# Layer-norm statistics at the ends of sub-layers on ScalarE and GpSimd, and all weight splits on VectorE

## Chip, cores and metric
The kernel runs on one core of a Trainium2 chip. The metric is device microseconds of one execution, a median over several runs. A core has TensorE (PE, matrix products), VectorE (DVE), ScalarE (ACT) and GpSimd (POOL), each with its own instruction stream that runs in order, and SyncE (SP), which here starts the DMA transfers. An instruction waits on semaphores that the other engines raise.

## What is computed
An encoder of four layers over 512 tokens of width 1024, in float32. Each layer is a token mixer (multi-head latent attention MLA, retention, gated linear attention GLA, MLA again) and a SwiGLU FFN, and each of these eight sub-layers ends in a layer norm:

```python
def layer_norm(x, g, b):
    mu = jnp.mean(x, axis=-1, keepdims=True)
    var = jnp.mean(jnp.square(x - mu), axis=-1, keepdims=True)
    return (x - mu) * lax.rsqrt(var + LN_EPS) * g + b

for i in range(DEPTH):
    y = mixer[i % 3](x, ...)
    x = layer_norm(DEEPNORM_ALPHA * x + y, ln_g[i, 0], ln_b[i, 0])
    x = layer_norm(DEEPNORM_ALPHA * x + swiglu_ffn(x, ...), ln_g[i, 1], ln_b[i, 1])
```

## The kernel before
**Products.** A float32 product is made of three faster ones: each operand is split into a high half (rounded, a copy on ScalarE, L102) and a low half (the difference, a subtraction, L103), and `mm3` (L127 to L130) multiplies high by high, high by low and low by high. Weights stream from HBM in pieces of 128x1024 elements (`wraw`), which `wsplit` splits into `whi` and `wlo`. The activations `x` lie as four token tiles `xt0` to `xt3` of 128x1024, and transposed as `xh` and `xl`.

**End of a sub-layer.** `out_proj` makes the last projection tile by tile: for each token tile two halves of 512 columns, each summed in PSUM and added into `xt` by `acc` (L182 or L184). In the last pass `acc` also takes the statistics of the half (`bn_stats`, L186). When both halves are there, `ln_finish` aggregates them (L191), takes the reciprocal root of the variance in eight steps on 128x1 operands (`rsqrt`, L141 to L149; it can be given an engine, and GpSimd already runs it for the RMS norms), and normalises with two operations per half (L205, L206). In the tail (last layer) the second half of tiles 0 to 2 goes through ScalarE (L200) and GpSimd (L201, L202) and then out.

A finished tile is put on a list. `flush` takes it off later, in the middle of the products of a following tile: eight transposes on TensorE (L158), then `xh` on ScalarE and `xl` on VectorE. The next sub-layer begins with projections of these.

**Where weights are split.** After each end, `self.relieve = 6` makes the next six weight pieces have their low half computed by GpSimd; inside GLA there are three more times two. All others are on VectorE.

**Order.** The instructions of each engine are laid in an order by a scheduler when the program is built; the program's own order is only its input. So what stands in front of what is read from the built program. Buffers come from pools (`b=10` is the number of general 128x512 buffers in the FFN's phase).

Of the kernel before, what the change touches and what calls it, by code (L numbers as in the profile page):

```python
# [9 lines left out]
F32 = mybir.dt.float32  # L10
F32R = mybir.dt.float32r
I32 = mybir.dt.int32
AF = mybir.ActivationFunctionType
ALU = mybir.AluOpType
AX = mybir.AxisListType

P = 128
D = 1024
S = 512
NT = S // P  # L20
# [3 lines left out]
LN_EPS = 1e-5  # L24
# [26 lines left out]
class Trunk:  # L51
    def __init__(self, tc, ctx, ins, nb=47, nraw=3, nhl=6):
        self.tc, self.nc, self.ins = tc, tc.nc, ins
        nc = tc.nc
        ctx.enter_context(nc.allow_non_contiguous_dma(reason="rows of weights and broadcasts"))
        pool = lambda name, bufs, **k: ctx.enter_context(tc.tile_pool(name=name, bufs=bufs, **k))
        self.cp = pool("cp", 1)
        self.wp = pool("wp", 1)
        self.nb = nb
        self.sp = pool("sp", 8)  # L60
        self.lnp = pool("lnp", 2)

        xp = pool("xp", 1)
        self.xh = xp.tile([P, KT, S], F32R, name="xh")
        self.xl = xp.tile([P, KT, S], F32R, name="xl")
        self.ps_pool = pool("psum", 6, space=bass.MemoryType.PSUM)
        self.nraw, self.nhl = nraw, nhl
        self.relieve = 0
        self.pending = []
        self.waiting = []  # L70

        self.ident = self.cp.tile([P, P], F32, name="ident")
        make_identity(nc, self.ident)
        self.xt = [self.cp.tile([P, D], F32, name=f"xt{t}") for t in range(NT)]
# [23 lines left out]
        return self.b(shape, F32R, "bh", tag), self.b(shape, F32R, "bl", tag)  # L98


    def split(self, hi, lo, src, eng=None):
        a = self.nc.scalar.copy(hi, src)  # L102
        b = (eng or self.nc.vector).tensor_tensor(lo, src, hi.bitcast(F32), op=ALU.subtract)  # L103
        return a.ins, b.ins

    def wload(self, srcs, a, n):
# [9 lines left out]
    def wsplit(self, raw, a, n):  # L116
        hi = self.wp.tile([P, a, n], F32R, tag="whi", name="whi", bufs=self.nhl)
        lo = self.wp.tile([P, a, n], F32R, tag="wlo", name="wlo", bufs=self.nhl)
        self.split(hi, lo, raw, self.nc.gpsimd if self.relieve > 0 else None)
        self.relieve -= 1  # L120
        return hi, lo

    def wcols(self, w, r0, kt, c0, n):
# [46 lines left out]
    def ln_begin(self, i, k):  # L170
        nc = self.nc
        self.g = self.lnp.tile([P, D], F32, tag="ln", name="ln_g")
        self.bb = self.lnp.tile([P, D], F32, tag="ln", name="ln_b")
        nc.sync.dma_start(self.g, self.ins["ln_g"][i, k].partition_broadcast(P))
        nc.sync.dma_start(self.bb, self.ins["ln_b"][i, k].partition_broadcast(P))
        self.stats = [self.small(12, "lnst") for _ in range(NT)]

    def acc(self, t, half, ps, coef, last):
        nc = self.nc
        x = self.xt[t][:, half * 512 : half * 512 + 512]  # L180
        if coef is None:
            nc.vector.tensor_tensor(x, ps, x, op=ALU.add)  # L182
        else:
            nc.vector.scalar_tensor_tensor(x, x, coef, ps, op0=ALU.mult, op1=ALU.add)  # L184
        if last:
            nc.vector.bn_stats(self.stats[t][:, half * 6 : half * 6 + 6], x)  # L186

    def ln_finish(self, t, out=None):
        nc = self.nc
        mv = self.small(2, "lnmv")  # L190
        nc.vector.bn_aggr(mv, self.stats[t].rearrange("p (a b) -> p a b", b=6))  # L191
        r = self.rsqrt(mv[:, 1:2], 1.0, LN_EPS, "ln")
        x = self.xt[t]
        for hf in range(2):
            sl = slice(hf * 512, hf * 512 + 512)
            if out is not None and t < NT - 1 and hf == 1:

                nb = self.small(1, "lnnb")
                nc.vector.scalar_tensor_tensor(nb, mv[:, 0:1], -1.0, r, op0=ALU.mult, op1=ALU.mult)
                nc.scalar.activation(x[:, sl], x[:, sl], AF.Identity, bias=nb, scale=r)  # L200
                nc.gpsimd.tensor_tensor(x[:, sl], x[:, sl], self.g[:, sl], op=ALU.mult)  # L201
                nc.gpsimd.tensor_tensor(x[:, sl], x[:, sl], self.bb[:, sl], op=ALU.add)  # L202
                nc.sync.dma_start(out[t * P : (t + 1) * P, sl], x[:, sl])
                continue
            nc.vector.scalar_tensor_tensor(x[:, sl], x[:, sl], mv[:, 0:1], self.g[:, sl], op0=ALU.subtract, op1=ALU.mult)  # L205
            nc.vector.scalar_tensor_tensor(x[:, sl], x[:, sl], r, self.bb[:, sl], op0=ALU.mult, op1=ALU.add)  # L206
            if out is not None:
                nc.sync.dma_start(out[t * P : (t + 1) * P, sl], x[:, sl])
        if out is None:
            self.pending.append(t)  # L210


    def out_proj(self, st, w, nf, coef, last, out=None, halves=(0, 1)):
        wf = lambda f0, half: self.wcols(w, f0 * P, 2, half * 512, 512)
        if nf <= 6:
            ch = {(c, hf): wf(2 * c, hf) for hf in halves for c in range(nf // 2)}
            for t in range(NT):
                for hf in halves:
                    ps = self.ps()
                    for f in range(nf):  # L220
                        if last and hf == 0 and f == 3:
                            self.flush(t - 2)
                        w2 = ch[f // 2, hf]
                        self.mm3(ps, st(f, t), (w2[0][:, f % 2, :], w2[1][:, f % 2, :]), f == 0, f == nf - 1)
                    self.acc(t, hf, ps, coef, last)
                if last:
                    self.ln_finish(t, out)
            self.relieve = 6 if last else 0
            return
        pss = [self.ps() for _ in range(NT)]  # L230
        for f in range(nf):
            if f % 2 == 0:
                w2 = wf(f, 0)
            for t in range(NT):
                self.mm3(pss[t], st(f, t), (w2[0][:, f % 2, :], w2[1][:, f % 2, :]), f == 0, f == nf - 1)
        for t in range(NT):
            self.acc(t, 0, pss[t], coef, last)
        self.out_tail(st, lambda f0: wf(f0, 1), nf, coef, last, out)

    def out_tail(self, st, wf, nf, coef, last, out=None):  # L240

        pss = [self.ps() for _ in range(NT)]
        nl = 8
        for f in range(nf - nl):
            if f % 2 == 0:
                w2 = wf(f)
            for t in range(NT):
                self.mm3(pss[t], st(f, t), (w2[0][:, f % 2, :], w2[1][:, f % 2, :]), f == 0, False)
        ch = [wf(nf - nl + 2 * c) for c in range(nl // 2)]
        for t in range(NT):  # L250
            for c in range(nl):
                if last and c == 3:
                    self.flush(t - 2)
                f = nf - nl + c
                w2 = ch[c // 2]
                self.mm3(pss[t], st(f, t), (w2[0][:, c % 2, :], w2[1][:, c % 2, :]), f == 0, f == nf - 1)
            self.acc(t, 1, pss[t], coef, last)
            if last:
                self.ln_finish(t, out)
        self.relieve = 6  # L260


    def proj_f(self, w2, ps, kt, m, c=slice(None), mid=None):
# [674 lines left out]
    def gla(self, l, j):  # L938
        nc = self.nc
# [77 lines left out]
        def silu(r):  # L1017
            for x in r:
                self.silu = self.tc.keep_in_program_order(nc.scalar.activation(x, x, AF.Silu))
# [3 lines left out]
        v, r, hs = first()  # L1023
# [13 lines left out]
        for h in range(GLA_H):  # L1037
            at, states = self._gla_scores(c, keys, v, fwd, crs)
            if h < 2:
                if h:  # L1040
                    qk["q", h + 2] = q(h + 2)
                qk["k", h + 2] = k(h + 2)
            else:
                out(0, yT[:4], False, (h - 2,))
            self._gla_mix(at, states, c[2:], v, r, ng)
            r0 = r
            if h + 1 < GLA_H:
                cs = gates(h + 1)
                c = self._gla_chain(cs, qk["q", h + 1], qk["k", h + 1])
                (v,) = project(values(h + 1))  # L1050
            yT += self._gla_turn(r0)
            if h + 1 < GLA_H:
                (r,) = project(gate(h + 1))
                self.relieve = 2
                keys = self._gla_keys(c)
                silu(r)
        out(1, yT[4:], True)
# [192 lines left out]
    def run(self, out):  # L1250
        self.load_x(self.ins["x"][0])
        for i in range(DEPTH):
            self.mixer(i)
            with self.phase(fh=8, ft=1, t=3, u=1, b=10):
                self.ffn(i, out[0] if i == DEPTH - 1 else None)


# [38 lines left out]
```

## Time and profile before

| what | value |
|---|---|
| median of 3 runs | 2599.5 us (2598.32 to 2600.16) |
| the profiled execution | 2595.45 us |
| its span in the profile | 2593.7 us |
| mean granted TensorE clock | 0.994 |
| busy: PE, DVE, ACT, POOL | 2536.9, 1792.7, 974.6, 335.7 us |
| chain that ended last | PE 85%, DVE 9%, ACT 2%, POOL 2%, issue 2%, DMA 1% |

The span is from the first to the last instruction of the profiled execution. Busy shares are means over stages with different limits, so one reads next which instructions TensorE waited before, and then the timeline of the engine that it waited for. A row of a timeline gives the start, the duration, the engine and line, output and inputs, and in brackets the idle time ahead of it with what ended it.

### The profile page before, as it was taken

The page shows a single profiled execution, that of the slowest core. Times are in us where ns is not written, and L with a number is a line of the kernel's source. Part 1 is how long each engine was busy: PE and PEld are TensorE (multiplying, and loading weights), DVE is VectorE, ACT ScalarE, POOL GpSimd, SP SyncE. Part 2 cuts the span into 40 slices and gives each one's busy share as a digit, 9 for nine tenths or more (in the row PEclk, how much of TensorE's full clock was granted, in tenths as well). Part 3 has the DMA queues.
Part 4 walks back from the last instruction along what each step waited for, and adds up shares of the span by engine and source line. Part 5 has one row for each costly group of instructions (what it writes and reads, how often), then busy time and mean ns, then how long its engine had stood idle before and what let it go on. Part 6 is the DMA issues. An engine that isn't in the chain of part 4 may idle for free.

```text
span 2593.7 us, 32609 instructions
## 1 busy us (share of the span) xinstructions
PE 2536.9 (98%) x12804; PEld 2156.5 (83%) x12804; DVE 1792.7 (69%) x2900; ACT 974.6 (38%) x1405; POOL 335.7 (13%) x359
## 2 busy tenths in 40 slices
PE   8999999999999999999999999999999999999998
PEld 6888888887888887988888998888888788888887
DVE  6877666668755648566657878866657586666656
ACT  4652333323333332333323665233332464233331
POOL 3002111002100103111102001211102200211101
PEclk9999999999999999999999999999999999999999
DMA  4213333323222323333333222333333221333331
GB/s 147 74 42 94 106 98 98 106 74 103 76 81 82 98 80 88 108 93 107 110 95 88 76 66 74 110 98 98 98 90 86 61 77 44 120 98 98 98 90 57
DMA packets 294714, 232.36 MB, mean 90 GB/s; under 512 B 21120, under 2 KB 244480, under 8 KB 294560
## 3 DMA queue, kind: packets, MB, share of 16 engines
q1 hardware_dynamic: 294560, 230.28, 29.4%
q8 instruction: 100, 1.64, 0.3%
q14 instruction: 54, 0.44, 0.1%
HBM read 228.15 MB, written 2.10 MB: 89 GB/s over the span
## 4 chain that ended last, share of the span: by engine, by line
PE 85%; DVE 9%; ACT 2%; POOL 2%; issue 2%; DMA 1%; DVEq 0%; SPq 0%; ACTq 0%; POOLq 0%
PE ps L128 27%; PE ps L130 27%; PE ps L129 27%; DVE xt L205 2%; DVE xt L206 1%; PE tp L658 1%; DVE lnst L186 1%; DVE lnu L145 1%; DVE xl L103 1%; PE tp L158 1%; DVE xt L182 1%; DVE bl L103 1%; PE ps L639 1%; PE ps L638 0%; DVE wlo L103 0%
## 5 line engine op out<-in xcount | busy, mean ns | idle before, releaser
L102 ACT CAST whi<-wraw 128x1024 fp32r<-128x1024 f32 (+3 forms) x398 | 412.2, 1040 | 700.3 <-issue 261.3
L129 PE MATMUL ps<-xl,whi 128*128 128x512 f32 (+1 forms) x1792 | 660.3, 368 | 8.1 <-DVE xl L103 8.1
L128 PE MATMUL ps<-xh,whi 128*128 128x512 f32 (+1 forms) x1792 | 660.4, 369 | 0.0
L130 PE MATMUL ps<-xh,wlo 128*128 128x512 f32 (+1 forms) x1792 | 659.3, 368 | 0.0
L103 DVE TENSOR_TENSOR wlo<-wraw,whi 128x1024 fp32r<-128x1024 f32 (+2 forms) x350 | 430.5, 1240 | 203.9 <-ACT whi L102 196.5
L129 PEld LDWEIGHTS ps<-xl,whi 128*128 128x128 f32 x1792 | 341.1, 190 | 64.1 <-DVE xl L103 9.3
L130 PEld LDWEIGHTS ps<-xh,wlo 128*128 128x128 f32 x1792 | 341.1, 190 | 55.0
L128 PEld LDWEIGHTS ps<-xh,whi 128*128 128x128 f32 x1792 | 340.9, 190 | 54.8 <-issue 0.4
L130 PE MATMUL ps<-whi,xl 128*128 128x512 f32 (+3 forms) x752 | 263.7, 351 | 5.1 <-DVE xl L103 5.1
L128 PE MATMUL ps<-whi,xh 128*128 128x512 f32 (+3 forms) x752 | 265.7, 353 | 0.7 <-ACT xh L102 0.7
L129 PE MATMUL ps<-wlo,xh 128*128 128x512 f32 (+3 forms) x752 | 263.2, 350 | 2.0 <-POOL wlo L103 2.0
L103 POOL TENSOR_TENSOR wlo<-wraw,whi 128x1024 fp32r<-128x1024 f32 (+4 forms) x48 | 118.0, 2474 | 912.1 <-ACT whi L102 900.6
L182 DVE TENSOR_TENSOR xt<-ps,xt 128x512 f32<-128x512 f32 x288 | 187.2, 682 | 35.8 <-PE ps L130 35.8
L128 PE MATMUL ps<-whi,fh 128*128 128x512 f32 x448 | 174.3, 389 | 0.0
L129 PE MATMUL ps<-wlo,fh 128*128 128x512 f32 x448 | 174.3, 389 | 0.0
L130 PE MATMUL ps<-whi,fl 128*128 128x512 f32 x448 | 174.3, 389 | 0.0
L130 PEld LDWEIGHTS ps<-whi,xl 128*128 128x128 f32 x752 | 143.5, 191 | 23.2 <-DVE xl L103 6.1
L129 PEld LDWEIGHTS ps<-wlo,xh 128*128 128x128 f32 x752 | 143.7, 191 | 19.1 <-POOL wlo L103 2.2
L128 PEld LDWEIGHTS ps<-whi,xh 128*128 128x128 f32 x752 | 143.8, 191 | 18.4 <-ACT xh L102 1.1
L326 DVE TENSOR_TENSOR ft<-ps,b 128x512 f32<-128x512 f32 x64 | 44.2, 691 | 142.5 <-PE ps L130 78.1
L102 ACT CAST whi<-wt 128x1024 fp32r<-128x1024 f32 x64 | 67.5, 1054 | 191.0 <-PE ps L129 128.4
L329 POOL TENSOR_TENSOR ft<-ft 128x256 f32<-128x256 f32 x32 | 23.6, 737 | 821.8 <-DVE ft L326 821.8
(249 smaller groups left out, 4135.7 us busy)
## 6 DMA issues: line engine op xcount, KB each, us to landing
wraw<-in_ffn_w_in SPq DMA_DIRECT2D x176, 512.0 KB, 3.9
wt<-in_ffn_w_out SPq DMA_DIRECT2D x48, 512.0 KB, 4.8
wraw<-in_ret_w_in SPq DMA_DIRECT2D x48, 512.0 KB, 3.9
wraw<-in_ffn_w_out SPq DMA_DIRECT2D x40, 512.0 KB, 3.4
wraw<-in_gla_w_in SPq DMA_DIRECT2D x22, 512.0 KB, 3.6
wraw<-in_mla_w_o SPq DMA_DIRECT2D x16, 512.0 KB, 3.8
wraw<-in_ret_w_o SPq DMA_DIRECT2D x16, 512.0 KB, 4.5
wraw<-in_mla_w_down SPq DMA_DIRECT2D x8, 512.0 KB, 4.3
```

What stands on the lines that cost most here:

```text
L102: a = self.nc.scalar.copy(hi, src)
L103: b = (eng or self.nc.vector).tensor_tensor(lo, src, hi.bitcast(F32), op=ALU.subtract)
L128: mm(out, s[0], m[0], start=start, stop=False)
L129: mm(out, s[0], m[1], start=False, stop=False)
L130: mm(out, s[1], m[0], start=False, stop=stop)
L145: stt(u, y, y, x, op0=ALU.mult, op1=ALU.mult)
L158: nc.tensor.transpose(ps[:, j, :], self.xt[t][:, (4 * g + j) * P : (4 * g + j + 1) * P], self.ident)
L182: nc.vector.tensor_tensor(x, ps, x, op=ALU.add)
L186: nc.vector.bn_stats(self.stats[t][:, half * 6 : half * 6 + 6], x)
L205: nc.vector.scalar_tensor_tensor(x[:, sl], x[:, sl], mv[:, 0:1], self.g[:, sl], op0=ALU.subtract, op1=ALU.mult)
L206: nc.vector.scalar_tensor_tensor(x[:, sl], x[:, sl], r, self.bb[:, sl], op0=ALU.mult, op1=ALU.add)
L326: nc.vector.tensor_tensor(ft[:, 2:4, :] if f % 2 else ft[:, 1::-1, :], half(pu), half(s), op=ALU.mult)
```

## The change
Three things change.

1. `relieve` is gone: the low half of every weight piece is subtracted on VectorE. 48 such instructions move from GpSimd.
2. For token tiles 0 to 2 of every end the statistics are no longer `bn_stats` and `bn_aggr` on VectorE. ScalarE sums the two halves (`Copy` with an accumulator, into a junk tile), GpSimd makes the mean and its negative, ScalarE sums the squares of the halves with the negative mean as bias, GpSimd adds the two sums and runs the eight steps of the root. Tile 3 stays as it was. The variance is formed from the same centred squares.
3. The FFN's phase has 9 general buffers in place of 10.

```diff
     def wsplit(self, raw, a, n):
...
-        self.split(hi, lo, raw, self.nc.gpsimd if self.relieve > 0 else None)
-        self.relieve -= 1
+        self.split(hi, lo, raw)
...
-        if last:
-            nc.vector.bn_stats(self.stats[t][:, half * 6 : half * 6 + 6], x)
+        if last and t == NT - 1:
+            nc.vector.bn_stats(self.stats[:, half * 6 : half * 6 + 6], x)
...
     def ln_finish(self, t, out=None):
+        x = self.xt[t]
         mv = self.small(2, "lnmv")
-        nc.vector.bn_aggr(mv, self.stats[t].rearrange("p (a b) -> p a b", b=6))
-        r = self.rsqrt(mv[:, 1:2], 1.0, LN_EPS, "ln")
-        x = self.xt[t]
+        if t == NT - 1:
+            nc.vector.bn_aggr(mv, self.stats.rearrange("p (a b) -> p a b", b=6))
+            r = self.rsqrt(mv[:, 1:2], 1.0, LN_EPS, "ln")
+        else:
+
+            ss = self.small(4, "lnss")
+            nb = self.small(1, "lnnm")
+            ts = nc.gpsimd.tensor_scalar
+            for n in range(4):
+                if n == 2:
+                    ts(mv[:, 0:1], ss[:, 0:1], ss[:, 1:2], 1.0 / D, op0=ALU.add, op1=ALU.mult)
+                    ts(nb, mv[:, 0:1], -1.0, None, op0=ALU.mult)
+                half = x[:, n % 2 * 512 : n % 2 * 512 + 512]
+                junk = self.lnp.tile([P, 512], F32, tag="lnj", name="ln_j", bufs=1)
+                if n < 2:
+                    nc.scalar.activation(junk, half, AF.Copy, accum_out=ss[:, n : n + 1])
+                else:
+                    nc.scalar.activation(junk, half, AF.Square, bias=nb, accum_out=ss[:, n : n + 1])
+            ts(ss[:, 2:3], ss[:, 2:3], ss[:, 3:4], None, op0=ALU.add)
+            r = self.rsqrt(ss[:, 2:3], 1.0 / D, LN_EPS, "lnp", nc.gpsimd)
...
-            self.relieve = 6 if last else 0
...
-        self.relieve = 6
...
-                self.relieve = 2
...
-            with self.phase(fh=8, ft=1, t=3, u=1, b=10):
+            with self.phase(fh=8, ft=1, t=3, u=1, b=9):
```

In the changed kernel the lines have other numbers: L102 is a split's subtraction, L180 and L182 are `acc`, L184 and L191 the statistics, L139 to L147 the root, L205 and L207 ScalarE's sums and squares, L221 and L222 the two normalising operations, L215 to L218 the tail's second half. The built order shows what moved.

VectorE at the first MLA end, from the second L205 of tile 0 (`xt_80`) to the last accumulation and statistics of tile 1 (`xt_81`), before:

```order
L205 SCALAR_TENSOR_TENSOR xt_80<-xt_80,lnmv,ln_g 128x512
L145 SCALAR_TENSOR_TENSOR lnu<-lny,lnx 128x1
L146 SCALAR_TENSOR_TENSOR lnu<-lnu 128x1
L147 SCALAR_TENSOR_TENSOR lny<-lnu,lny 128x1
L148 SCALAR_TENSOR_TENSOR lnu<-lny,lnm 128x1
L149 SCALAR_TENSOR_TENSOR lny<-lnu,lny 128x1
L206 SCALAR_TENSOR_TENSOR xt_80<-xt_80,lny,ln_b 128x512 x2
L184 SCALAR_TENSOR_TENSOR xt_81<-xt_81,ps 128x512
L186 BN_STATS lnst<-xt_81 128x6
```

And in the changed kernel, from tile 0's last accumulation to tile 2 (`lnpy` is the root that GpSimd makes):

```order
L182 SCALAR_TENSOR_TENSOR xt_80<-xt_80,ps 128x512
L221 SCALAR_TENSOR_TENSOR xt_80<-xt_80,lnmv,ln_g 128x512 x2
L222 SCALAR_TENSOR_TENSOR xt_80<-xt_80,lnpy,ln_b 128x512 x2
L182 SCALAR_TENSOR_TENSOR xt_81<-xt_81,ps 128x512
L221 SCALAR_TENSOR_TENSOR xt_81<-xt_81,lnmv,ln_g 128x512 x2
L102 TENSOR_TENSOR xl<-tp,xh 128x4x128
L222 SCALAR_TENSOR_TENSOR xt_81<-xt_81,lnpy,ln_b 128x512 x2
L102 TENSOR_TENSOR xl<-tp,xh 128x4x128
L182 SCALAR_TENSOR_TENSOR xt_82<-xt_82,ps 128x512
L102 TENSOR_TENSOR wlo<-wraw,whi 128x1024
L221 SCALAR_TENSOR_TENSOR xt_82<-xt_82,lnmv,ln_g 128x512
L102 TENSOR_TENSOR xl<-tp,xh 128x4x128
```

The accumulation of tile 1 stood behind a chain that was all VectorE's own; now it stands behind L222 of tile 0, which needs GpSimd's root, and a weight split (`wlo`) stands among the operations of tile 2.

ScalarE at the same end, before (`xh<-tp` are the copies of the transposed tiles):

```order
L102 CAST xh<-ps 128x512
L102 CAST whi<-wraw 128x1024
L102 CAST xh<-tp 128x4x128 x2
L102 CAST whi<-wraw 128x1024
L102 CAST xh<-tp 128x4x128 x2
L102 CAST whi<-wraw 128x1024 x3
```

And in the changed kernel:

```order
L101 CAST whi<-wraw 128x1024
L205 ACTIVATE ln_j,lnss<-xt_80 128x512
L207 ACTIVATE ln_j,lnss<-xt_80,lnnm 128x512 x2
L205 ACTIVATE ln_j,lnss<-xt_81 128x512 x2
L207 ACTIVATE ln_j,lnss<-xt_81,lnnm 128x512 x2
L101 CAST xh<-tp 128x4x128 x2
L205 ACTIVATE ln_j,lnss<-xt_82 128x512 x2
L101 CAST whi<-wraw 128x1024
L207 ACTIVATE ln_j,lnss<-xt_82,lnnm 128x512
L101 CAST xh<-tp 128x4x128
L207 ACTIVATE ln_j,lnss<-xt_82,lnnm 128x512
L101 CAST xh<-tp 128x4x128
```

Four activations per tile came in between, and the second square of tile 2 (`xt_82`) stands behind a copy of tile 1's transposes.

VectorE in the tail, from the last normalising operation of tile 2 (`xt_82`) to tile 3's (`xt_83`) statistics, before:

```order
L149 SCALAR_TENSOR_TENSOR lny<-lnu,lny 128x1
L206 SCALAR_TENSOR_TENSOR xt_82<-xt_82,lny,ln_b 128x512
L199 SCALAR_TENSOR_TENSOR lnnb<-lnmv,lny 128x1
L182 TENSOR_TENSOR xt_83<-ps,xt_83 128x512
L186 BN_STATS lnst<-xt_83 128x6
L182 TENSOR_TENSOR xt_83<-ps,xt_83 128x512
L186 BN_STATS lnst<-xt_83 128x6
L191 BN_AGGR lnmv<-lnst 128x2
```

And in the changed kernel:

```order
L221 SCALAR_TENSOR_TENSOR xt_82<-xt_82,lnmv,ln_g 128x512
L180 TENSOR_TENSOR xt_83<-ps,xt_83 128x512
L222 SCALAR_TENSOR_TENSOR xt_82<-xt_82,lnpy,ln_b 128x512
L215 SCALAR_TENSOR_TENSOR lnnb<-lnmv,lnpy 128x1
L184 BN_STATS lnst<-xt_83 128x6
L180 TENSOR_TENSOR xt_83<-ps,xt_83 128x512
L184 BN_STATS lnst<-xt_83 128x6
L191 BN_AGGR lnmv<-lnst 128x2
```

Both accumulations of tile 3 stand there; the second one is behind L222 of tile 2. On GpSimd the mean of tile 2 (L200) stands behind both products of tile 1 (L217, L218):

```order
L147 TENSOR_SCALAR lnpy<-lnpu,lnpy 128x1
L217 TENSOR_TENSOR xt_81<-xt_81,ln_g 128x512
L218 TENSOR_TENSOR xt_81<-xt_81,ln_b 128x512
L200 TENSOR_SCALAR lnmv<-lnss 128x1
L201 TENSOR_SCALAR lnnm<-lnmv 128x1
L208 TENSOR_SCALAR lnss<-lnss 128x1
```

Before, GpSimd had only such products (L201, L202) in the tail.

## Rows read from the trace of the kernel before

**Rows 1.** the page's busy time, share of the span and instructions of each engine:
```profile
PE 2536.9 (98%) x12804; PEld 2156.5 (83%) x12804; DVE 1792.7 (69%) x2900; ACT 974.6 (38%) x1405; POOL 335.7 (13%) x359
```

**Rows 2.** TensorE's waits by line: for what, us in total, times, longest:
```profile
PE tp L158 <- DVE xt L206: 8.6, 5, 3.6
...
PE ps L129 <- DVE xl L103: 8.1, 4, 3.4
```

**Rows 3.** timeline (start us, us, engine, operation [idle before]): TensorE, three ends:
```profile
614.33 0.80 PE L130 MATMUL ps<-whi,xl 128*128 128x512 f32 x1 [4.91 <-DVE xl L103]
...
1612.92 0.44 PE L1234 MATMUL tp<-ident,b 128*128 128x128 f32 x2 [2.31 <-DVE b L1227]
...
1650.45 1.29 PE L158 MATMUL tp<-ident,xt 128*128 128x128 f32 x8 [3.62 <-DVE xt L206]
```

**Rows 4.** timeline of VectorE, then GpSimd, at the first MLA end, 234 to 246:
```profile
234.50 0.74 DVE L205 SCALAR_TENSOR_TENSOR xt<-xt,lnmv,ln_g 128x512 f32<-128x512 f32 x1
...
235.23 2.83 DVE L205 SCALAR_TENSOR_TENSOR xt<-xt,lnmv,ln_g 128x512 f32<-128x512 f32 x1
...
242.55 0.68 DVE L103 TENSOR_TENSOR xl<-tp,xh 128x512 fp32r<-128x512 f32 x1
...
234.75 10.18 POOL L103 TENSOR_TENSOR wlo<-wraw,whi 128x1024 fp32r<-128x1024 f32 x4 [16.17 <-ACT whi L102]
```

**Rows 5.** timeline of TensorE at the first MLA end:
```profile
227.78 1.04 PE L158 MATMUL tp<-ident,xt 128*128 128x128 f32 x8
...
234.12 1.03 PE L158 MATMUL tp<-ident,xt 128*128 128x128 f32 x8
...
240.94 0.39 PE L129 MATMUL ps<-xl,whi 128*128 128x256 f32 x1 [2.25 <-DVE xl L103]
```

**Rows 6.** a stretch: us, busy of PE, PEld, DVE, ACT, POOL, then granted clock, DMA:
```profile
242.00:245.40 3.40, 3.15 (x16) 2.86 (x15) 3.32 (x5) 0.23 (x1) 2.93 (x2) 0.50 0.89 260
```

**Rows 7.** groups by line and shape: count | busy us, mean ns | idle before:
```profile
L103 POOL TENSOR_TENSOR wlo<-wraw,whi 128x1024 fp32r<-128x1024 f32 x42 | 106.1, 2542 | 800.6 <-ACT whi L102 790.3 <-DVE xt L184 9.0 <-PE tp L901 1.1
...
L103 DVE TENSOR_TENSOR wlo<-wraw,whi 128x1024 fp32r<-128x1024 f32 x339 | 422.1, 1255 | 196.0 <-ACT whi L102 188.7
...
L205 DVE SCALAR_TENSOR_TENSOR xt<-xt,lnmv,ln_g 128x512 f32<-128x512 f32 x61 | 62.0, 1025 | 0.0
```

**Rows 8.** timeline of VectorE, tile 0 of the first MLA end, no split beside:
```profile
220.50 0.69 DVE L184 SCALAR_TENSOR_TENSOR xt<-xt,ps 128x512 f32<-128x512 f32 x1 [2.53 <-PE ps L130]
...
224.79 1.42 DVE L206 SCALAR_TENSOR_TENSOR xt<-xt,lny,ln_b 128x512 f32<-128x512 f32 x2
...
226.12 0.68 DVE L184 SCALAR_TENSOR_TENSOR xt<-xt,ps 128x512 f32<-128x512 f32 x1
```

**Rows 9.** timeline of VectorE, ScalarE and GpSimd in the tail:
```profile
2576.91 0.69 DVE L182 TENSOR_TENSOR xt<-ps,xt 128x512 f32<-128x512 f32 x1 [2.25 <-PE ps L130]
...
2585.07 0.69 DVE L182 TENSOR_TENSOR xt<-ps,xt 128x512 f32<-128x512 f32 x1 [2.25 <-PE ps L130]
...
2573.36 0.82 ACT L200 ACTIVATE xt<-xt,lnnb,lny 128x512 f32<-128x512 f32 x1 [7.34 <-DVE lnnb L199]
...
2574.26 1.29 POOL L201 TENSOR_TENSOR xt<-xt,ln_g 128x512 f32<-128x512 f32 x1 [5.48 <-ACT xt L200]
```

**Rows 10.** groups of ScalarE by shape: an activation of 128x512 that sums:
```profile
L645 ACT ACTIVATE b<-ps,mx 128x512 f32<-128x512 f32 x64 | 43.8, 687 | 55.5 <-DVE mx L642 55.3
...
L645 ACT ACTIVATION_READ_ACCUMULATOR b<-ps,mx 128x1 f32 x64 | 12.5, 195 | 0.0
```

**Rows 11.** timeline of GpSimd, first and last step of two of 16 roots:
```profile
2017.57 0.19 POOL L141 TENSOR_SCALAR rmsx<-ssq 128x1 f32<-128x1 f32 x1 [5.19 <-ACT b L510]
...
2020.03 0.26 POOL L149 TENSOR_SCALAR rmsy<-rmsu,rmsy 128x1 f32<-128x1 f32 x1
...
42.03 0.55 POOL L141 TENSOR_SCALAR rmsx<-ssq 128x1 f32<-128x1 f32 x1 [1.55 <-ACT b L510]
...
46.63 0.26 POOL L149 TENSOR_SCALAR rmsy<-rmsu,rmsy 128x1 f32<-128x1 f32 x1
```

More of the change, by code (lines that the diff above doesn't have):

```diff
@@ L67, in __init__ @@
         self.nraw, self.nhl = nraw, nhl
-        self.relieve = 0
         self.pending = []
@@ L98, in bpair, with split @@
         return self.b(shape, F32R, "bh", tag), self.b(shape, F32R, "bl", tag)
-    def split(self, hi, lo, src, eng=None):
+    def split(self, hi, lo, src):
         a = self.nc.scalar.copy(hi, src)
-        b = (eng or self.nc.vector).tensor_tensor(lo, src, hi.bitcast(F32), op=ALU.subtract)
+        b = self.nc.vector.tensor_tensor(lo, src, hi.bitcast(F32), op=ALU.subtract)
         return a.ins, b.ins
@@ L175, in ln_begin @@
         nc.sync.dma_start(self.bb, self.ins["ln_b"][i, k].partition_broadcast(P))
-        self.stats = [self.small(12, "lnst") for _ in range(NT)]
+        self.stats = self.small(12, "lnst")
     def acc(self, t, half, ps, coef, last):
```

## The prediction
> **What bounds the kernel now.** I read the profile in this order. The busy shares first: TensorE works 2536.9 us of the 2593.7 us span (98%) and VectorE 69% [rows 1]. So a change to VectorE, ScalarE and GpSimd can only move the places where TensorE waits for them. The list of TensorE's waits says where those are: 8.6 us before transposes that want a normalised tile (`tp` on `xt` of L206), 8.1 us before products that want the low half of the transposed activations (`xl`) [rows 2], and single waits of 4.91, 2.31 and 3.62 us at the end of an FFN, in GLA and at its end [rows 3]. All of them stand at the ends of sub-layers. There are eight ends (MLA, FFN, retention, FFN, GLA, FFN, MLA, FFN); the eighth has nothing behind it and is the tail.
>
> Then the cause. At the first MLA end VectorE runs the two L205 of a tile in 0.74 us each, until GpSimd starts four weight splits at 234.75 that take 10.18 us. From then on one L205 takes 2.83 us [rows 4]. TensorE, waiting for `xl` behind these, stands still for 2.25 us [rows 5], and its granted clock is 0.50, the lower of its two levels (1.2 of 2.4 GHz), for the next 3.4 us [rows 6]. At that level TensorE covers half the work, so I price one such stretch at 1.5 to 1.7 us. The mean L205 is 1.025 us against 0.74 undisturbed [rows 4, 7].
>
> **Part 1, the 48 splits move from GpSimd to VectorE.** 42 of them have the full size: 2.54 us on GpSimd, 1.255 us on VectorE [rows 7]. Six per end make 6 × 1.255 = 7.5 us of new VectorE work. What it gives back: at the MLA end the L205 beside a split loses 2.83 − 0.74 = 2.1 us [rows 4], and if each of the four splits holds up one VectorE instruction alike, 8.4 us in all. VectorE's sum is a draw. What differs is order: a split on VectorE waits in line, and a TensorE product that needs that low half waits with it.
>
> The Trainium skill ("SBUF — State Buffer", section "SBUF: two separate sides") says that VectorE and GpSimd share one port pair, which whoever starts first holds for a whole instruction, against a VectorE operation with two SBUF inputs if the GpSimd one reads SBUF. The 2.83 us beside a 2.5 us split agrees with it [rows 4]. It speaks for this part, and against the next: by the rule each of the 264 new GpSimd operations would contend for the same lock with VectorE's L205, L206 and splits.
>
> **Part 2, statistics of tiles 0 to 2.** Off VectorE per tile: two statistics, one aggregate, eight root steps. In their place, four 128x512 activations on ScalarE and eleven 128x1 operations on GpSimd; 24 tiles, so 96 and 264 instructions. Neither engine is short of time; what counts is the latency from the tile's last accumulation to its last L206. Before, undisturbed: the accumulation starts at 220.50 and ends at 221.19, the L206 pair ends at 224.79 + 1.42 = 226.21, so **5.0 us** [rows 8]. After, added up from rows:
> - a hop from ScalarE to GpSimd: 2573.36 + 0.82 to 2574.26, 0.08 us [rows 9]; I take 0.1 for each of five hops, 0.5;
> - the sum of the second half: 0.69 us and a read-out of 0.19 that partly overlaps [rows 10], 0.75 to 0.88, taken 0.75;
> - mean and its negative: two small GpSimd operations; the eight of a quiet root (next point but one) average 0.34, so 0.7 at most, and 0.45 if both are as short as its first ones (0.19); taken 0.45;
> - two squares, 1.5 to 1.76, taken 1.5;
> - the sum of squares and the root: a root of eight such operations takes 2017.57 to 2020.03 + 0.26 = 2.72 us when VectorE is quiet, and 42.03 to 46.63 + 0.26 = 4.86 us when it isn't [rows 11]; taken 2.72, since in the new order VectorE mostly stands waiting for this very root, plus 0.3 for the addition;
> - the L206 pair, 1.42.
>
> Sum 7.6 us (to 8.3), so **+2.6 us of latency** for each of the three tiles (bounds +2.5 from the smallest values and +5.4 with the loud root).
>
> A second effect comes from the order: in the mixers' ends the last accumulation of tile t + 1 stands behind L222 of tile t, which waits for GpSimd's root. So the tiles no longer overlap; the delays add up from tile to tile. ScalarE's queue adds a third: the tile's second square stands behind the copies `xh` of the tile before, which wait for TensorE's transposes. Table loads stay 21.
>
> **End by end.** *First MLA end.* Tile 0 is ready at 221.2 + 7.6 = 228.8 in place of 226.2; its transposes start at 227.78 [rows 5], and the first four need only the first half (0.7 us earlier), so TensorE waits some 0.7. The accumulation of tile 1, at 226.12 before [rows 8], now stands behind tile 0 and starts at 228.8: 2.7 late. Tile 1 is ready at 228.8 + 0.7 + 7.6 = 237.1; its transposes, at 234.12 before [rows 5], are due at 234.8 now; the first half is there at 236.4 and the second at 237.1, so with the four transposes between them 1.9 of wait. Tile 2: accumulation behind that and one `xl` at 237.8, ready at 237.8 + 0.7 + 7.6 + 0.7 (a copy in between on ScalarE) = 246.8. The second `xl` of tile 1 stands behind it and is done at 247.5; before it was done at 242.55 + 0.68 = 243.2 [rows 4]. The first FFN pair, which wants both parts, therefore waits twice, about 1.8 and 3.1. Together 7.5 us, against about 4.2 before (2.25, a fraction of a us, 1.6 for the clock): **+3.3**. The second MLA end has the same code and gets the same: +6.6 for both.
>
> *Tail.* A tile takes 2585.07 − 2576.91 = 8.16 us of TensorE [rows 9]. The mean of tile t + 1 now stands on GpSimd behind two products of 1.29 us of tile t [rows 9], which wait for tile t's root. From an accumulation's end the cycle is 0.75 + 0.45 + 1.5 + 0.3 + 2.72 + 0.75 (one L222) + 0.82 + 2.6 = 9.9 us before hops, longer than 8.16. The lag grows over tiles 1 and 2, and the last accumulation of tile 3, at 2585.07 before, stands behind L222 of tile 2; I get 2588.1 for it: **+3.0**, and nothing after it to hide it. Bounds +2 and +6 by the two roots.
>
> *Retention's end.* The order on VectorE and ScalarE is the MLA end's, on a stretch whose wait for `xl` was longer before; I take a third of the MLA end's price, +1.0 (0 to +3.3).
>
> *The three FFN ends inside.* A tile of 8.16 us covers 7.6 us, so the roots are hidden. Gone is the 4.91 us wait that ends at 614.33 [rows 3]; what comes instead is a split, now behind tile 2's L222, which TensorE wants some 2.3 us before. I take −0.2 for the three (−6 to +4).
>
> *GLA.* The wait of 2.31 us at 1612.92 is for a VectorE result of GLA's own small roots while GpSimd has two splits; I read it as held up by these, and let it go, and the one of 3.62 at 1650.45 is shortened [rows 3], less the longer chain: −2.5 (−5 to 0). The other splits inside GLA cost nothing: TensorE doesn't wait there, its products of the heads hide them; without that cover each would cost 1.255.
>
> *Clock.* There are more waits of 2 to 3 us than before, in clusters, and such waits were followed by stretches at the lower level: one or two more, +2 (0 to +5).
>
> **Sum.** 6.6 + 3.0 + 1.0 − 0.2 − 2.5 + 2.0 = **+9.9 us**. The profiled run took 2595.45 us, 1.75 more than its span, and lies 4 us under the median of 2599.5, so I add the difference to the median: 2609.4. Its own range, by the smaller bounds, is 2604.7 to 2615.
>
> **Rivals.** *A, faster: the freed VectorE decides.* All the waits in the list of TensorE's waits and the single ones are behind stretched VectorE instructions: 8.6 + 8.1 and the 4.91 [rows 2, 3], and half-clock stretches of 1.6 us after the long ones [rows 6]. If TensorE finds tile 2's and tile 3's data early because splits no longer hold VectorE, a third to a half of some 25 us and of six or seven stretches comes back while the tail costs 3: −6 to −13, near 2589. It decides if the roots come before TensorE asks; for it speak the FFN ends with 8.16 against 7.6, against it the MLA ends, where a tile takes 6.3.
>
> *B, no difference: the gains in GLA and the FFN ends (up to −11) meet the MLA ends and the tail.* 2599, within 5 either way.
>
> *C, much slower: the lock.* If GpSimd's roots run as at 42.03 (4.86) [rows 11], each of the 24 tiles is 2.1 us later than I take. It decides if VectorE has splits or L221 to run beside a root. In the ends where tiles queue behind each other this goes through two or three times: 4 ends × some 3 us and the tail's 3: +12 on top, near 2622. By the rule of the Trainium skill ("SBUF — State Buffer", section "SBUF: two separate sides") this is what a root beside VectorE's two-input work would meet.
>
> *D, the change doesn't do what it says:* the diff takes the splits' engine argument away altogether, and the new order has 48 more splits on VectorE, so I give it nothing.
>
> **How the numbers follow.** A difference under 0.2%, 5.2 us, can't be told from none. Forecast (+5.2 to +15): 0.45. C and mixtures with it (over +15): 0.19. B: 0.19. A: 0.17. So slower 0.64, same 0.19, faster 0.17. The range reaches into A as far as −6.5 and into C as far as +23: 2593 to 2622.5, with some 0.12 below and 0.06 above.
>
> **What would show it.** Right: L221 and L222 at 0.74 nearly everywhere; GpSimd roots at 2.7; the last accumulation of tile 1 at an MLA end starting at the end of tile 0's L222; in the tail, the accumulation of tile 3 some 3 us after TensorE's last product. Wrong: no wait for GpSimd ahead of L222 (A), roots over 4 us (C), or TensorE's waits for `wlo` of VectorE at the FFN ends, which would mean that part 1 costs what I put on part 2.

## The result and the profile after

The changed kernel takes 2618.74 us (median of 6 runs, 2614.94 to 2621.93) against 2599.53 us of the kernel before on the same chip. The ratio is 1.0081, with a 95% interval of 1.0071 to 1.0091: slower by 0.8%, 19 us. Slower was forecast, with 2609.4 us and a range of 2593.0 to 2622.5, so the time lies in the range but the loss is twice the 9.9 us forecast. The profiled execution took 2617.96 us with a span of 2616.2 us, 22.5 us more than before; that is more than the 19 us of the medians because the profiled execution of the kernel before lies 4 us under its median.

The busy line and TensorE's longest waits (engine, tile and line, what it waited for, us in total, times, longest) of the changed kernel, which answer to [rows 1] and [rows 2]:

```profile
PE 2546.9 (97%) x12804; PEld 2162.5 (83%) x12804; DVE 1717.8 (66%) x2684; ACT 1044.0 (40%) x1597; POOL 298.0 (11%) x575
...
PE tp L156 <- DVE xt L222: 17.3, 9, 2.9
PE ps L127 <- DVE wlo L102: 10.3, 5, 3.3
PE ps L127 <- DVE xl L102: 6.4, 2, 3.3
```

VectorE is 75 us less busy, as the change meant it to be, and TensorE waits longer for it: 17.3 us in place of 8.6 for a normalised tile, and 10.3 us for low halves of weights, a wait that VectorE did not cause before. VectorE's own waits (the same columns) say why. It stands for 59.4 us with L222 at the head of its queue until GpSimd has a root, and 39.7 us until ScalarE has its sums:

```profile
DVE xt L222 <- POOL lnpy L147: 59.4, 24, 3.0
DVE xt L221 <- ACT ln_j L207: 39.7, 17, 4.6
```

The timelines at the first MLA end (VectorE, then ScalarE, GpSimd and TensorE) answer to [rows 4], [rows 5] and [rows 8]:

```profile
220.59 0.69 DVE L182 SCALAR_TENSOR_TENSOR xt<-xt,ps 128x512 f32<-128x512 f32 x1 [2.90 <-PE ps L128]
...
223.66 1.60 DVE L221 SCALAR_TENSOR_TENSOR xt<-xt,lnmv,ln_g 128x512 f32<-128x512 f32 x2 [2.38 <-ACT ln_j L207]
...
228.27 1.41 DVE L222 SCALAR_TENSOR_TENSOR xt<-xt,lnpy,ln_b 128x512 f32<-128x512 f32 x2 [3.01 <-POOL lnpy L147]
229.60 0.68 DVE L182 SCALAR_TENSOR_TENSOR xt<-xt,ps 128x512 f32<-128x512 f32 x1
...
239.18 0.68 DVE L182 SCALAR_TENSOR_TENSOR xt<-xt,ps 128x512 f32<-128x512 f32 x1
...
222.82 0.72 ACT L207 ACTIVATE ln_j<-xt,lnnm 128x512 f32<-128x512 f32 x1 [0.72 <-POOL lnnm L201]
...
223.66 0.73 ACT L207 ACTIVATE ln_j<-xt,lnnm 128x512 f32<-128x512 f32 x1
...
224.58 0.84 POOL L208 TENSOR_SCALAR lnss<-lnss 128x1 f32<-128x1 f32 x1 [1.80 <-ACT ln_j L207]
225.51 0.19 POOL L139 TENSOR_SCALAR lnpx<-lnss 128x1 f32<-128x1 f32 x1
...
227.97 0.27 POOL L147 TENSOR_SCALAR lnpy<-lnpu,lnpy 128x1 f32<-128x1 f32 x1
...
238.14 2.29 PE L156 MATMUL tp<-ident,xt 128*128 128x128 f32 x8 [2.28 <-DVE xt L222]
...
249.21 0.58 PE L127 MATMUL ps<-xl,whi 128*128 128x256 f32 x1 [3.32 <-DVE xl L102]
```

From the accumulation's end (221.28) to the last L222 (229.68) are 8.4 us, 5.0 before. The accumulations of tiles 0, 1 and 2 start at 220.59, 229.60 and 239.18: 9.0 and 9.6 us apart, on a stretch where TensorE needs 6.3 us for a tile. At this end nothing stretches VectorE any more (L221 has a mean of 0.77 us over the kernel); it waits. Around these two waits TensorE's granted clock is at its lower level (0.50) for 3.4 and 6.8 us (one 3.4 us stretch before, [rows 6], whose columns these rows have):

```profile
237.90:241.30 3.40, 3.07 (x11) 2.51 (x12) 1.96 (x4) 1.35 (x3) 0.44 (x2) 0.50 0.00 0
248.20:255.00 6.80, 5.79 (x27) 5.79 (x28) 6.80 (x13) 0.00 (x0) 0.00 (x0) 0.50 0.34 96
```

At an FFN end the row that answers to the first of [rows 3] is a wait for a weight's low half, and VectorE's rows beside it show that the split stands behind L222, an `xl` and an accumulation:

```profile
608.93 0.50 PE L127 MATMUL ps<-wlo,xh 128*128 128x512 f32 x1 [3.28 <-DVE wlo L102]
...
605.13 1.42 DVE L222 SCALAR_TENSOR_TENSOR xt<-xt,lnpy,ln_b 128x512 f32<-128x512 f32 x2 [2.35 <-POOL lnpy L147]
606.46 0.69 DVE L102 TENSOR_TENSOR xl<-tp,xh 128x512 fp32r<-128x512 f32 x1
607.06 0.69 DVE L180 TENSOR_TENSOR xt<-ps,xt 128x512 f32<-128x512 f32 x1
607.65 1.22 DVE L102 TENSOR_TENSOR wlo<-wraw,whi 128x1024 fp32r<-128x1024 f32 x1
```

In the tail (VectorE, then GpSimd; compare [rows 9]) the mean of tile 2 waits for both products of tile 1, and the last accumulation of tile 3 stands behind L222 of tile 2:

```profile
2605.12 0.75 DVE L222 SCALAR_TENSOR_TENSOR xt<-xt,lnpy,ln_b 128x512 f32<-128x512 f32 x1 [2.69 <-POOL lnpy L147]
...
2606.46 0.67 DVE L180 TENSOR_TENSOR xt<-ps,xt 128x512 f32<-128x512 f32 x1
...
2608.28 1.83 DVE L221 SCALAR_TENSOR_TENSOR xt<-xt,lnmv,ln_g 128x512 f32<-128x512 f32 x1
...
2598.22 1.29 POOL L218 TENSOR_TENSOR xt<-xt,ln_b 128x512 f32<-128x512 f32 x1
2599.62 0.26 POOL L200 TENSOR_SCALAR lnmv<-lnss 128x1 f32<-128x1 f32 x1
```

To see where the time goes, one mark serves for all kernels: the start of tile 3's transposes at each end, and TensorE's last product. Between two marks the same products run, so the difference to the kernel before is what that stretch gained or lost (worked out from the traces, us, profiled executions). The columns behind "after" are the experiments e1, e4, e5, e6, e7 and e8 of the next section; the profiled executions of the kernel before and of e5 lie 4 us under their medians, so differences of up to 4 us in the last row mean nothing:

```
stretch up to      before     after   splits  mixers' ends  roots on  root on   short   half of
                   mark at    - before only   old           VectorE   GpSimd    root    splits
MLA end 1           255.12    +7.5    -2.1    -3.0          -3.3      +2.4      +0.9    -0.9
FFN end 1           618.88    -1.8    -6.2    -1.1          -7.2      -4.4      -6.4    -4.4
retention end      1048.55    +1.9    -5.3    -4.6          -4.5      +1.9      -4.6    -6.5
FFN end 2          1406.88    +4.1    -2.9    +2.2          -2.7      +2.1      -0.8    -0.8
GLA end            1658.82    -5.4   -10.9   -10.9          -8.5      -6.2     -11.7    -5.8
FFN end 3          2017.46    +0.9    -6.8    -1.6          -3.6      -2.0      -4.4    -3.4
MLA end 2          2245.42    +9.9    +0.6    -2.1          -4.4      +5.0      +0.7    -3.9
last product       2585.03     0.0     0.0     0.0           0.0       0.0       0.0     0.0
tail               2593.68    +5.3     0.0    +5.3          +0.7       0.0       0.0     0.0
span               2593.68   +22.5   -33.6   -15.8         -33.6      -1.3     -26.3   -25.6
```

### The profile page after: what moved, and what is told of

It is laid out like the page before. It is cut to its first block, busy times and chain, and to the rows that moved or that the text cites. A ratio compares the mean times of both kernels' runs of the same rounds, so it can differ in the third digit from the quotient of the medians.

```text
span 2616.2 us, 32909 instructions
## 1 busy us (share of the span) xinstructions
PE 2546.9 (97%) x12804; PEld 2162.5 (83%) x12804; DVE 1717.8 (66%) x2684; ACT 1044.0 (40%) x1597; POOL 298.0 (11%) x575
## 4 chain that ended last, share of the span: by engine, by line
PE 83%; POOL 5%; DVE 4%; issue 3%; ACT 3%; DMA 1%; ACTq 0%; DVEq 0%; SPq 0%; POOLq 0%
PE ps L126 27%; PE ps L127 27%; PE ps L128 27%; ACT ln_j L207 1%; DVE xt L222 1%; PE tp L672 1%; ACT ln_j L205 1%; PE ps L653 1%; DVE wlo L102 1%; POOL lnss L208 1%; PE ps L652 1%; DVE xt L180 1%; DMA wraw<-in_mla_w_down 0%; PE tp L156 0%; DVE xl L102 0%
## 5 line engine op out<-in xcount | busy, mean ns | idle before, releaser
L102 DVE TENSOR_TENSOR wlo<-wraw,whi 128x1024 fp32r<-128x1024 f32 (+3 forms) x398 | 487.0, 1232 | 219.8 <-ACT whi L101 212.6
L127 PE MATMUL ps<-wlo,xh 128*128 128x512 f32 (+3 forms) x752 | 264.9, 353 | 10.4 <-DVE wlo L102 10.3
L180 DVE TENSOR_TENSOR xt<-ps,xt 128x512 f32<-128x512 f32 x288 | 187.0, 683 | 27.7 <-PE ps L128 27.7
L102 DVE TENSOR_TENSOR fl<-ft,fh 128x1792 fp32r<-128x1792 f32 x32 | 64.8, 2026 | 93.0 <-ACT fh L101 93.0
L126 PE MATMUL ps<-bh 128*128 128x256 f32 (+1 forms) x376 | 123.3, 334 | 2.6 <-ACT bh L101 2.3
```

What stands on the lines that cost most here:

```text
L102: b = self.nc.vector.tensor_tensor(lo, src, hi.bitcast(F32), op=ALU.subtract)
L126: mm(out, s[0], m[0], start=start, stop=False)
L127: mm(out, s[0], m[1], start=False, stop=False)
```

## The experiments

**All splits on VectorE, statistics as before (e1).** Part 1 of the change alone.

```diff
-        self.split(hi, lo, raw, self.nc.gpsimd if self.relieve > 0 else None)
-        self.relieve -= 1
+        self.split(hi, lo, raw)
```

> The kernel before with part 1 alone: all low halves on VectorE, statistics as before. Theory (the new statistics' latency is what costs, the moved splits are a small gain): in the comparison of starts of the same TensorE products, GLA gives back some 5 us as in the changed kernel, the MLA ends give back up to 2 each, the FFN ends stay within 2; 2590 to 2596 us. Rival (the moved splits cost: TensorE waits for low halves that stand in VectorE's line): waits for wlo of 3 us at three FFN ends stay, and the time is 2605 or more.

Measured: 2560.73 us, ratio to before 0.9852 (0.9838 to 0.9867), and 2560.87 us when it was run again later. Both expected ranges were missed: the splits alone are worth 38 us. The new statistics must then cost 2618.7 − 2560.7 = 58 us. The busy line, TensorE's waits and the group of the first normalising operation (L204 here), the counterpart of the one in [rows 7]:

```profile
PE 2530.8 (99%) x12804; PEld 2152.6 (84%) x12804; DVE 1771.2 (69%) x2948; ACT 976.3 (38%) x1405; POOL 222.2 (9%) x311
...
PE tp L530 <- DVE b L521: 4.6, 2, 2.6
...
PE tp L530 <- DVE b L515: 3.3, 2, 1.9
PE ps L129 <- DVE xl L103: 2.4, 2, 1.6
...
L204 DVE SCALAR_TENSOR_TENSOR xt<-xt,lnmv,ln_g 128x512 f32<-128x512 f32 x61 | 44.7, 742 | 0.0
```

VectorE took over 48 splits and is yet 21.5 us less busy than before (1792.7 to 1771.2): its operations with two inputs in SBUF are no longer held up. Of TensorE's waits for `xl` 2.4 us are left, 1.6 of them at 30 us, ahead of the first end, and there is none for a low half of a weight; apart from the first load, the longest waits now are for the RMS norms of MLA. The four half-clock stretches ahead of the tail (20.5 us in sum, 27 before) follow these waits; none lies at an end.

**The new statistics, splits on GpSimd as before (e2).** Part 2 alone (`wsplit` and `relieve` as in the kernel before).

```diff
+        self.split(hi, lo, raw, self.nc.gpsimd if self.relieve > 0 else None)
+        self.relieve -= 1
-        self.split(hi, lo, raw)
...
```

> The changed kernel with part 1 undone: the 48 splits are on GpSimd again, the statistics of tiles 0 to 2 stay on ScalarE and GpSimd. Theory: at least as slow as the changed kernel, 2618 to 2628 us, since GpSimd's roots now also stand behind splits of 2.5 us. Rival (the splits cost): near the kernel before, 2598 to 2604 us.

Measured: 2646.76 us, ratio 1.0184 (1.0169 to 1.0199), 48 us over the kernel before beside it. The rival falls, and the theory's sign holds, though its size was short here too. GpSimd's timeline at the first MLA end shows the addition of the squares of tile 2 (L210) behind a split:

```profile
245.06 2.41 POOL L103 TENSOR_TENSOR wlo<-wraw,whi 128x1024 fp32r<-128x1024 f32 x1 [0.35 <-ACT whi L102]
247.46 0.71 POOL L210 TENSOR_SCALAR lnss<-lnss 128x1 f32<-128x1 f32 x1
```

So part 2 costs 48 us with the splits on GpSimd and 58 us with them on VectorE; part 1 is worth 38 us with the old statistics and 28 us with the new ones.

**The tail's statistics as before (e3).** In the last `ln_begin` a flag sends tiles 0 to 2 to VectorE's statistics.

```diff
-        self.ln_begin(l, 1)
+        self.ln_begin(l, 1, out is not None)
...
-        if last and t == NT - 1:
+        if last and (self.old or t == NT - 1):
...
```

> The changed kernel with the statistics of the last end alone (the tail) as before. Theory: the end after TensorE's last product falls from 13.9 us back to 8.7 us, so 5 us less than the changed kernel: 2613 to 2614 us. If the tail's lag came from TensorE's own delay, it stays near 2618.7.

Measured: 2613.51 us, 5.2 less than the changed kernel. The tail's 5.3 us in the table is the tail's own lag.

**The mixers' statistics as before (e4).** The same flag in the four mixers' ends; FFN ends and tail keep the new statistics.

```diff
-            self.ln_begin(l, 0)
+            self.ln_begin(l, 0, True)
...
```

> The changed kernel with the statistics of the four mixers' ends as before; FFN ends and tail keep the new ones. Theory (in the mixers' ends the tiles queue behind each other's roots, 7.7 us in each MLA end and 2 in retention's): 14 to 19 us less than the changed kernel, 2600 to 2605 us. Rival (the splits cost): no more than 3 us less, 2616 or more.

Measured: 2578.22 us, 40.5 less than the changed kernel, where 14 to 19 were expected. The theory's place is right and the rival falls. The size is larger because with the old statistics these ends also show what the splits give. Against the splits alone, the three FFN ends of this kernel lose 5.1, 5.1 and 5.2 us (the table's rows) and the tail 5.3: so the new statistics cost about 5 us at each FFN end too. What TensorE waits for there is a weight's low half, in all three:

```profile
PE ps L127 <- DVE wlo L102: 10.0, 3, 3.4
```

The same splits stand on VectorE in e1, where this wait does not exist. So it comes from L222, which holds the split up while it waits for GpSimd's root.

**Mean and root on VectorE, sums on ScalarE (e5).**

```diff
-            ts = nc.gpsimd.tensor_scalar
+            ts = nc.vector.tensor_scalar
...
-            r = self.rsqrt(ss[:, 2:3], 1.0 / D, LN_EPS, "lnp", nc.gpsimd)
+            r = self.rsqrt(ss[:, 2:3], 1.0 / D, LN_EPS, "lnp")
```

> The changed kernel with the mean and the root of tiles 0 to 2 on VectorE; ScalarE still makes the sums. The chain from a tile's last accumulation to its last L222, 8.4 us in the changed kernel at the first MLA end, becomes some 7.0 (eight root steps in about 1.5 in place of 2.7, and no hop before L222). Theory (what costs is the length of that chain against a tile's TensorE time of 6.3 to 8.2 us): about 20 us less than the changed kernel, 2590 to 2605 us. Rival (GpSimd's part costs next to nothing, the two passes of ScalarE are the cost): 2612 us or more.

Measured: 2566.18 us, ratio to before 0.9878 (0.9861 to 0.9894): 52.6 us less than the changed kernel, where about 20 were expected. Having the eleven small operations on GpSimd is nine tenths of what part 2 costs. For ScalarE's two passes and for the nine buffers of the third part, which was not tried alone, 5.5 us are left together (2566.2 against 2560.7), and the two ratios' intervals overlap. VectorE's timeline at the first MLA end shows what it does in place of waiting: the next tile's accumulation (L182) runs ahead of L222, and everything that waits in the queue moves.

```profile
220.75 0.69 DVE L182 SCALAR_TENSOR_TENSOR xt<-xt,ps 128x512 f32<-128x512 f32 x1 [2.90 <-PE ps L128]
...
226.54 0.16 DVE L147 SCALAR_TENSOR_TENSOR lnpy<-lnpu,lnpy 128x1 f32<-128x1 f32 x1
226.62 0.68 DVE L182 SCALAR_TENSOR_TENSOR xt<-xt,ps 128x512 f32<-128x512 f32 x1
227.22 1.41 DVE L222 SCALAR_TENSOR_TENSOR xt<-xt,lnpy,ln_b 128x512 f32<-128x512 f32 x2
...
232.97 0.68 DVE L182 SCALAR_TENSOR_TENSOR xt<-xt,ps 128x512 f32<-128x512 f32 x1
```

The chain is 7.2 us (221.44 to 228.63), near the 7.0 expected and still longer than TensorE's tile of 6.3 us. But the accumulations are only 5.9 and 6.4 us apart, where the changed kernel has 9.0 and 9.6. So what counts is not the chain's length by itself but whether VectorE stands still in it, and the next tile's accumulation with it: the next kernel has a shorter chain and costs far more.

**Only the root on GpSimd (e6).** The kernel of e1 with VectorE's statistics and the eight root steps of tiles 0 to 2 on GpSimd.

```diff
...
-        r = self.rsqrt(mv[:, 1:2], 1.0, LN_EPS, "ln")
+        r = self.rsqrt(mv[:, 1:2], 1.0, LN_EPS, "ln", nc.gpsimd if t < NT - 1 else None)
```

> The kernel of the first experiment (all splits on VectorE) with only the root of tiles 0 to 2 moved to GpSimd; statistics stay on VectorE. The chain is 0.7 + 0.2 + 2.8 + 1.4 with two hops, some 5.5 us, 0.5 over that of VectorE alone and below every tile's 6.3 us. Theory (a chain shorter than the tile costs nothing but in the tail): 2560 to 2568 us. Rival (each hop to GpSimd and the waiting VectorE cost by themselves, whatever the length): 2580 us or more.

Measured: 2595.79 us, ratio to before 0.9987 (0.9978 to 0.9997), 35 us over e1. The theory that a chain shorter than TensorE's tile is free falls; the time is in the rival's range. The timelines of VectorE, GpSimd and TensorE at the first MLA end:

```profile
221.46 0.69 DVE L183 SCALAR_TENSOR_TENSOR xt<-xt,ps 128x512 f32<-128x512 f32 x1 [1.41 <-PE ps L129]
...
226.91 1.42 DVE L205 SCALAR_TENSOR_TENSOR xt<-xt,lny,ln_b 128x512 f32<-128x512 f32 x2 [2.34 <-POOL lny L148]
228.24 0.68 DVE L183 SCALAR_TENSOR_TENSOR xt<-xt,ps 128x512 f32<-128x512 f32 x1
...
235.02 1.28 DVE L103 TENSOR_TENSOR xl<-tp,xh 128x512 fp32r<-128x512 f32 x2
236.22 0.68 DVE L183 SCALAR_TENSOR_TENSOR xt<-xt,ps 128x512 f32<-128x512 f32 x1
...
242.98 1.28 DVE L103 TENSOR_TENSOR xl<-tp,xh 128x512 fp32r<-128x512 f32 x2
...
223.21 0.75 POOL L140 TENSOR_SCALAR lnx<-lnmv 128x1 f32<-128x1 f32 x1 [161.85 <-DVE lnmv L190]
224.04 0.58 POOL L141 TENSOR_SCALAR lnm<-lnmv 128x1 f32<-128x1 f32 x1
...
243.72 0.39 PE L128 MATMUL ps<-xl,whi 128*128 128x256 f32 x1 [3.14 <-DVE xl L103]
```

The chain is 6.2 us (222.15 to 228.33), not 5.5: the first two root steps take 0.75 and 0.58 us while VectorE has L204 (223.15 to 224.56). But the period is longer than the chain. Each tile's VectorE work is chain, accumulation and two `xl`, and since VectorE stands still for 2.34 us in the chain, these come on top: the accumulations are 6.8 and 8.0 us apart (221.46, 228.24, 236.22) where TensorE needs 6.3. The two `xl` of tile 1 stand behind L205 of tile 2, and TensorE waits 3.14 us for them. The rival's "whatever the length" is not shown by this; the next run speaks against it.

**A root of two steps (e7).** The changed kernel with the first guess of the root alone, 2 of 8 steps on GpSimd. It leaves out the six steps that refine the guess, so its results are not the model's, and it serves for the time alone.

```diff
-            r = self.rsqrt(ss[:, 2:3], 1.0 / D, LN_EPS, "lnp", nc.gpsimd)
+            v, r = self.small(1, "lnpx"), self.small(1, "lnpy")
+            ts(v, ss[:, 2:3], 1.0 / D, LN_EPS, op0=ALU.mult, op1=ALU.add)
+            ts(r.bitcast(I32), v.bitcast(I32), -0.5, float(0x5F3759DF), op0=ALU.mult, op1=ALU.add)
```

> The changed kernel with two of the eight root steps on GpSimd (the first guess alone, so the normalisation of tiles 0 to 2 is a few per cent off). The chain falls from 8.4 to some 6.2 us, just under a tile's 6.3. Theory: most of what the new statistics cost (56 us by the first experiment) goes, 2575 to 2592 us. Rival (the order in which VectorE waits is the cost, whatever the length): 2608 us or more.

Measured: 2569.72 us, 49 less than the changed kernel and below the expected 2575 to 2592; the rival falls. VectorE's two waits (compare those of the changed kernel above):

```profile
DVE xt L223 <- ACT ln_j L207: 35.1, 16, 2.4
...
DVE xt L224 <- POOL lnpy L211: 16.0, 24, 1.0
```

The wait for ScalarE hardly changed (39.7 to 35.1 us), the wait for GpSimd fell from 59.4 to 16.0 us, and with it nearly all of the cost: the six small steps cost some 2 us on each of 24 tiles.

**Half of the splits on GpSimd (e8).** The kernel before with `relieve = 3` in place of 6, and 1 in place of 2.

> The kernel before with half of the splits on GpSimd: 3 per end and 1 in place of 2 inside GLA. Theory (each GpSimd split holds up VectorE's operations with two inputs in SBUF; the first ones fall into the last tile's normalisation and cost most): between the two, 2575 to 2590 us. Rival (only the last of the six reach into the next sub-layer's products): as the first experiment, 2560 to 2566 us.

Measured: 2569.41 us, ratio 0.989 (0.9875 to 0.9904), outside both expectations. Taking half of the splits off GpSimd gives 31 of the 38 us, which suggests that the later three of each six, the ones taken away, cost most. The table does not put this on one place, and no run takes away the first three, so this is not shown.

**The RMS norms' roots on VectorE too (e9).** Beside e1, run again on the same chip (e10).

```diff
...
-            return self.rsqrt(ss, 1.0 / n, RMS_EPS, "rms", nc.gpsimd)
+            return self.rsqrt(ss, 1.0 / n, RMS_EPS, "rms")
```

> The kernel of the first experiment (all splits on VectorE, statistics as before) with the roots of the two MLA layers' RMS norms moved from GpSimd to VectorE too. If a root on GpSimd costs through VectorE's wait in line, the four waits of TensorE for b of L515 and L521 (7.9 us in all) and the half-clock stretches behind them go: 4 to 9 us less than the first experiment, 2552 to 2557 us. If VectorE has no room there, the same or more than 2560 us.

> The kernel of the first experiment once more, beside the one with the RMS roots on VectorE on the same chip: 2558 to 2563 us.

Measured: 2552.55 us, ratio to before 0.9824 (0.981 to 0.9837), against 2560.87 us of e1 on the same chip: 8.3 us less, as expected. TensorE's waits for L515 and L521 fell from 7.9 us (4.6 + 3.3 in e1) to 1.5:

```profile
PE tp L530 <- DVE bl L537: 2.4, 2, 1.6
...
PE tp L530 <- DVE b L515: 1.5, 1, 1.5
```

This version beats both kernels, by 46 us the one before, measured beside it, and by some 66 us the changed one.

## Why the prediction was right in sign and short in size

- **What bounds the kernel.** Right: in every kernel TensorE has the same products, and the differences lie in its waits, in the half-clock stretches around them, and in the tail. But not all waits of the kernel before stand at the ends of sub-layers, as the prediction says. The 2.31 us in GLA lie 46 us ahead of its end, and 6.9 us for the RMS norms' results (3.6 for L522 and 3.3 for L516) are in the list of waits and not in the prediction; e9 gains 8.3 us there.
- **Part 1 as a draw.** This is the step that failed most. It was priced by VectorE's busy sum at one end, 7.5 us added against 8.4 given back, and the runs show −38 us. First, the sum set six splits against the hold-up of four. At the first MLA end four splits hold up the second L205 by 2.1 us and three steps of the root, which take 0.16 to 0.22 us undisturbed:

```profile
237.98 2.31 DVE L145 SCALAR_TENSOR_TENSOR lnu<-lny,lnx 128x1 f32<-128x1 f32 x1
...
240.81 1.81 DVE L146 SCALAR_TENSOR_TENSOR lnu<-lnu 128x1 f32<-128x1 f32 x1
...
243.15 1.79 DVE L147 SCALAR_TENSOR_TENSOR lny<-lnu,lny 128x1 f32<-128x1 f32 x1
```

That is 7.5 us given back for 4 × 1.255 = 5.0 us added. Over the kernel, VectorE had lost some 70 to 80 us to being held up: it is 21.5 us less busy in e1 after taking 48 splits of some 57 us in sum. Second, the sum is the wrong measure: the held-up operations stood in front of `xl` and of the last tile's normalisation, and with e1 nearly all of TensorE's waits at the ends go, and the half-clock stretches there with them. Rival A had just this mechanism, with −6 to −13 for the whole change; taken for part 1 alone and in full (some 25 us of waits and six or seven stretches of 1.6 us, some 35) it would have come near.
- **A sign that was misread in advance.** TensorE's waits for `wlo` of VectorE at the FFN ends did come, 3.3 us at each of three. The prediction would have taken them for a cost of part 1. e1 has the same splits in VectorE's queue and no such wait, so they belong to part 2.
- **Part 2, the latency.** The mechanism was right: L222 waits in line, the accumulations queue behind it, the tiles no longer overlap. The chain was put at 7.6 us and measured 8.4. The addition took 0.84 us in place of 0.3, with L221 of the same tile on VectorE at that moment, and the squares 0.84 each from start to start in place of 0.75. The root was 2.73 us (225.51 to 228.24), as taken, and all 24 lie between 2.72 and 3.14. So rival C's loud roots (4.86) did not come, although the time is nearer to its 2622 than to 2609.4. (Its own sum, 4 × 3 and the tail's 3, is +15 and not +12.) What part 2 costs with part 1 done was never priced apart; it is 58 us.
- **End by end.** MLA ends: +3.3 each and a share of the clock term, measured +7.5 and +9.9. The waits of 1.04, 2.28 and 3.32 us of TensorE are three of the four worked out (0.7, 1.9, 1.8 and 3.1); what was short is the clock, two stretches of 3.4 and 6.8 us in place of one of 3.4. The prediction's sum for this end has 1.6 us of clock on the side of before and none after. With both, it closes: 6.6 us of waits and half of 10.2 us, less 4.2, are +7.5. Of the second MLA end's +9.9 us some 2 lie earlier, where a 6.8 us half-clock stretch at 2060 has no counterpart before; what set it off is not known. Retention +1.0, measured +1.9. FFN ends −0.2 together, measured −1.8, +4.1 and +0.9: 8.16 us of TensorE's tile were to hide the roots, yet against e1 each loses 5 us (e4), through the split behind L222. That split was seen, with a wait of some 2.3 us; the wait is 3.3, with a half-clock stretch at each. GLA −2.5, measured −5.4. Tail +3.0, measured +5.3: the lag is 4.2, and 1.1 more come from L221 of tile 3, which takes 1.83 us beside a GpSimd product.
- **Clock.** +2.0 was for one or two more stretches. Leaving out the tails, there were 7 with 27 us in sum before and 10 with 48 us after; half of the 21 us is about +10, in place of the +2. TensorE's busy time for the same 12804 instructions agrees: 2536.9 us before and 2546.9 after. This is the term most short in the sum.
- **The shared port.** The prediction drew on the Trainium skill ("SBUF — State Buffer", section "SBUF: two separate sides") for the shared port pair that one of VectorE and GpSimd holds for a whole instruction. The traces agree in both directions: with the splits gone L204 takes 0.742 us on average in place of 1.025; and the small GpSimd operation beside L221 takes 0.84 us, the one beside L204 0.75, in place of 0.19 to 0.28.

That the sum was nearer than its terms is luck: two errors of opposite sign, −38 and +58 where 0 and about +10 were put.

## What to carry to other kernels

An engine's busy share alone does not say whether work should leave it: moving a chain of tiny dependent steps to an idle engine makes the busy one wait in line, and all that stands behind the wait is late; here eight steps of 128x1 cost 35 us on 24 tiles, though they took VectorE less than 2 us for each tile. Price a two-part change part by part, against the other part done and not done; a net of an end can hide two large terms. Work out the period of the waiting engine per tile (chain, waits and all else in its queue), not only the chain's length, and set that against the bounding engine's tile.

## What was not expected of the hardware

Beside GpSimd splits of 2.4 to 2.8 us at the first MLA end, a VectorE operation of 128x512 with two inputs in SBUF lost 2.1 us, and operations of 128x1 that take 0.16 to 0.22 us undisturbed lost 1.6 to 2.1 us, far more than their own length. Over 48 splits VectorE lost some 70 to 80 us, about 1.5 us for each. And waits of 2 to 3 us cost more than themselves: around the pair of 2.28 and 3.32 us at the first MLA end, TensorE ran for 10.2 us at the lower of its two clock levels (0.50).
